# The last triangular inverse moved beside the recurrence, and a layer's modulations moved from one filler to another

## The chip, the cores and the metric

The kernel runs on one core of one Trainium2 chip. The metric is the device time of one execution in microseconds (us). Engines are named as in the profile: PE (TensorE matmul), PEld (its weight load), DVE (VectorE), ACT (ScalarE), POOL (GpSimd) and SP (SyncE, here only a queue that issues transfers).

## The reference

The program is two blocks on 512 latent tokens and 256 context tokens of width 1024, in float32. The first block mixes three branches (window pooling, a differential attention, and a bidirectional recurrence called rwkv), merges them through gates, and ends in a mixture of experts. The second block has two layers: layer 0 is a long convolution (hyena) beside an mLSTM, layer 1 a latent attention, each with a feed-forward part. Each layer's norms and residuals are modulated by vectors computed from a conditioning vector. Cut to what matters here:

```python
def wkv_step(S, inp):                      # the recurrence, token by token
    r, w, k, v, a, b = inp
    sa = jnp.einsum('dbhvk,dbhk->dbhv', S, a)
    S = S * w[..., None, :] + sa[..., None] * b[..., None, :] + v[..., None] * k[..., None, :]
    return S, jnp.einsum('dbhvk,dbhk->dbhv', S, r)

def merge_branches(branches, gates, w_br, w_out):
    g = jax.nn.sigmoid(gates.reshape(B, L, N_BRANCH, D_MODEL))
    merged = g[:, :, 0] * (branches[0] @ w_br[0])
    for n in range(1, N_BRANCH):
        merged = merged + g[:, :, n] * (branches[n] @ w_br[n])
    return merged @ w_out

def ada_mod(cv, w, b):                     # the modulations: 1024 -> 6 * 1024
    m = jax.nn.silu(cv) @ w + b
    return jnp.split(m, N_MOD, axis=-1)
```

## The kernel before

Matrix products are made in float32 by splitting each operand into a high and a low part (names ending in h/hi and l/lo) and adding three products. A split is a cast on ACT and a difference on DVE.

Phase 1 makes the three branches. A first stage runs four generators woven together: `rwkv_inputs` (the recurrence's inputs for four chunks of two heads each), `attend` (the attention), `pools_gates` (pooling, then the modulations of the first block and of layer 0), and `rwkv_blocks`. The last of these inverts, for each chunk, the 32x32 triangular diagonal blocks: 31 steps, each a multiplication and a reduction on DVE over a growing square (`rwkv_block`), then two transposes whose results are stored to memory as `rw_inv`. A chunk's blocks are handed over in the list `todo` by the end of `rwkv_chunk_inputs`; the tiles (blkT, inv, blt, blkO) come from the pool of the recurrence's inputs. The steps of the first three chunks are paced by `PACE`; those of the fourth are not.

Then `rwkv` runs the recurrence: 24 units and 24 steps (four chunks of six pieces of 128 tokens), chunks 0 and 1 side by side and then 2 and 3. A unit (`rwkv_unit`) loads its inputs (ARl and BKl on SP's queue, X from `rw_inv` on POOL's) and prepares matrices that don't depend on the state; a step (`rwkv_step`) carries the state on. At most three units are ahead of the steps. Beside them runs `filler`: the 24 gate projections (`gates`, weights wg in pieces of four 128-row slices) and the merge of the first two branches (`merge_first`, matmuls mp, 16 units). The filler's progress is tied to the share of steps done: a gate i may start when 2 * i is not over `FILL` * (done / 24 + 0.1), a merge unit when 48 + 8 * b + n is not. The pools of the filler lie at the right end of the memory, where later x (the residual) and the second set of constants (const, vec) are put. After the recurrence `rwkv_out` normalises a chunk's result, and `merge` takes the third branch and the output projection.

The modulations are made by `ada_steps`: 96 loads of 256 KB (wada) for a whole layer, one matmul of 32 columns for each, four of them at a time into one PSUM bank, then a copy and eight small matmuls (adc). Those of layer 1 (`ada_w1`) run in `layer0` as the lowest stream beside the long convolution and the mLSTM, with 5 buffers.

The order of the work is decided in two steps. `weave` picks the next generator by a model of the clock in the program (`Clock`): among those whose inputs are modelled as ready, the one with the lowest rank; a stream of rank 2 goes first when the model sees PE too little active. The program's order is then the priority of a list scheduler, which gives each engine the first instruction that it holds to be ready, so the order on an engine can differ from the program's. Each engine and each queue of transfers then runs in that order.

Of the kernel before, what the change touches and what calls it, by code (L numbers as in the profile page):

```python
# [22 lines left out]
FT = mybir.dt.float32  # L23
# [394 lines left out]
class Builder:  # L418
# [288 lines left out]
    def phase1(self, es):  # L707
# [15 lines left out]
        self.fac = self.pool(es, "keep1").tile([128, 4, 2, 6, 2], FT, name="fac")  # L723
        with ExitStack() as e:
            self.h1s = ExitStack()
            hl = self.pool(self.h1s, "h1l", side="right")
            self.h1l = [hl.tile([128, 8, NL], FR, name=n) for n in ("h1l_hi", "h1l_lo")]
            with ExitStack() as e2:
                hc = self.pool(e2, "h1c")
                self.h1c = [hc.tile([128, 8, NCX], FR, name=n) for n in ("h1c_hi", "h1c_lo")]  # L730
                with ExitStack() as e3:
                    self.banks = dict(g=4, s=4)
                    self.psp = self.pool(e3, "psh", 1, space=PSUM)
                    self.head1(e3)
                self.banks = dict(g=3, f=2, s=2, h=1)
                self.psp = self.pool(e2, "ps0", 1, space=PSUM)
                self.lat, self.both = [(*self.h1l, 0, NL)], [(*self.h1c, 0, NCX), (*self.h1l, 0, NL)]
                with ExitStack() as e3, ExitStack() as e4:
                    self.todo = []
                    self.weave(*zip(self.RANKS, (self.rwkv_inputs(e3), self.attend(), self.pools_gates(e4), self.rwkv_blocks())))  # L740
            self.banks = dict(s=7, g=1)
            self.psp = self.pool(e, "ps2", 1, space=PSUM)
            self.rwkv(e)

# [54 lines left out]

    FILL = 64  # L800

    def filler(self, pace):

        with ExitStack() as e:
            yield from self.gates(e, range(self.GATES_A, 24), "g", 2, 4, pace, side="right")
        self.h1s.close()
        with ExitStack() as e:
            yield from self.merge_first(e, pace)

    def merge_first(self, es, pace):  # L810
# [52 lines left out]

    def ada_steps(self, wp, jobs, bufs=ADA):

# [11 lines left out]
        for w, s, L, X in jobs:  # L877
# [4 lines left out]
            nc.vector.tensor_copy(z[:, :, 2 * N - 2:2 * N], s)  # L882
            yield lambda: max(self.after(z), self.room("h"))
            p = self.ps("ada", "h")
            for n in range(N):
                for g in range(0, 8, 4):
                    while len(ahead) < bufs - 1 and todo:
                        load()
                    W = [ahead.pop(0) for _ in range(4)]
                    yield self.after(*W)  # L890
                    for j in range(4):
                        self.mm(p[32 * j:32 * j + 32], z[:, g + j, 2 * (N - 1 - n):2 * (N - 1 - n) + 32], W[j],
                                start=n + g == 0, stop=n == N - 1 and g == 4, skip_group_check=True)
# [322 lines left out]
    def rwkv_inputs(self, es):  # L1216
# [24 lines left out]
        nc.gpsimd.memset(blk, 0.0)  # L1241
        inv = wp.tile([128, 32, 32], FT, name="inv")
        nc.gpsimd.memset(inv, 0.0)
# [13 lines left out]
    def rwkv_chunk_inputs(self, c, proj, pp, W, blk, inv):  # L1257
# [100 lines left out]
        while self.todo:  # L1358
            yield self.later()
        A = pp.tile([128, 32, 32], FT, name="blkT", tag="blkT")  # L1360
        nc.vector.transpose(A, blk)
        self.todo.append((c, pp, A, inv))

    PACE = 1000.0

    def rwkv_blocks(self):

        for _ in range(4):
            while not self.todo:
                yield self.later()  # L1370
            yield from self.rwkv_block(*self.todo[0])
            self.todo.pop()

    def rwkv_block(self, c, pp, A, inv):
        nc = self.nc
        for i in range(1, 32):
            t = pp.tile([128, 31, 31], FT, name="blt", tag="blt")[:, :i, :i]
            nc.vector.tensor_mul(t, inv[:, :i, :i].rearrange("p m j -> p j m"), A[:, i, None, :i].to_broadcast([128, i, i]))
            nc.vector.tensor_reduce(inv[:, i, :i], t, op=OP.add, axis=AX.X)
            yield self.later(self.PACE if c < 3 else 0.0)  # L1380
        for z in range(2):
# [18 lines left out]

    def weave(self, *streams):

# [3 lines left out]
        n = len(S)  # L1406
        while S:
            now = self.clock.free.get("tensor", 0.0)
# [16 lines left out]

    def rwkv(self, es):
        nc = self.nc
# [9 lines left out]
        def units(q):  # L1437
            while todo:
                while made[0] - done[0] >= self.AHEAD:
                    yield self.later()  # L1440
                if todo:
                    c, n = todo.pop(0)
                    made[0] += 1
                    P = {}
                    yield from self.rwkv_unit(c, n, up, q, P)
                    ch[c, n] = P

# [19 lines left out]
        gens = [(0, steps(q)) for q in range(self.LANES)] + [(1, units(q)) for q in range(self.UNITS)]  # L1467
        self.weave(*gens, (2, self.filler(lambda: done[0] / 24 + 0.1)))

# [686 lines left out]
    def layer0(self, es):  # L2156
# [12 lines left out]
        with ExitStack() as e:  # L2169
            self.banks = dict(g=4, n=2, s=1, h=1)  # L2170
            self.psp = self.pool(e, "ps8", 1, space=PSUM)
            ada = self.ada_steps(self.pool(e, "adaw"), [(D["ada_w1"], self.s2, *self.mod2[1])])
            wp = self.pool(e, "ml")
            self.gates_made, self.heads_made, self.heads_out, self.ml, self.mo0, self.mo1, self.mixed = False, 0, 0, None, None, None, [False] * 2
            self.weave((1, self.l0_main()), (0, self.ml_main(wp)), (0, self.ml_heads(0)), (0, self.ml_heads(1)), (2, ada))
        self.dump("mo", self.mo)
# [794 lines left out]
```

## Time and profile before

| | us |
|---|---|
| median of 3 runs | 4022.8 |
| lowest and highest | 4019.8, 4026.1 |
| the profiled execution | 4023.9 |
| its span, first to last instruction | 4022.1 |
| PE busy | 3641.9 (91%) |
| DVE busy | 2487.6 (62%) |
| ACT busy | 1580.0 (39%) |
| mean granted clock of PE | 0.936 |

A busy share is an average over stages with different limits. A line of a timeline gives the start, the duration, the engine (a q behind it is its queue of transfers), the operation with output and input by the program's names, and in square brackets how long the engine sat idle before it and what ended that. The granted clock is 1.0 at 2.4 GHz and 0.5 at 1.2 GHz.

### The profile page before, as it was taken

Reading aid. Unit: us, or ns where it says so; the run is one execution under the profiler, and the core shown is the slowest. Engines: PE = TensorE matmul, PEld = TensorE weight load, DVE = VectorE, ACT = ScalarE, POOL = GpSimd, SP = SyncE. Lnnn points to the kernel's source line nnn. Section 1 sums busy time; section 2 is a strip of 40 time slices with the busy share of each in tenths; the row PEclk is TensorE's granted clock in tenths of the full one; section 3 lists DMA queues with packets and bytes.
Section 4 is the critical chain, followed back from the end, with each engine's and each line's share of the span. In section 5 each row is a group of like instructions: output and inputs, shape, how many; then the busy total and the mean of one; then the engine's idle time right before and its main releaser. Section 6 shows DMA issues by size and latency. Waiting matters only on the chain.

```text
span 4022.1 us, 50169 instructions
## 1 busy us (share of the span) xinstructions
PE 3641.9 (91%) x18332; PEld 2802.5 (70%) x18332; DVE 2487.6 (62%) x4564; ACT 1580.0 (39%) x2765; POOL 510.2 (13%) x742
## 2 busy tenths in 40 slices
PE   8998986898888689999989999899999999999998
PEld 4775443687777466666656886687888877667886
DVE  5597797877877468888874567445423344445343
ACT  3332332333332247666652653224313324434242
POOL 0222111322222021111110000110101000000010
PEclk9998896899888789999999999999999999999999
DMA  5224571322242649999953335312211210012332
GB/s 189 96 84 161 183 255 64 101 79 77 84 132 74 235 184 356 333 335 335 333 217 129 133 105 164 116 35 63 65 61 62 84 55 29 12 42 84 100 95 89
DMA packets 216781, 546.20 MB, mean 136 GB/s; under 512 B 41682, under 2 KB 63859, under 8 KB 189908
## 3 DMA queue, kind: packets, MB, share of 16 engines
q1 hardware_dynamic: 176848, 469.77, 34.1%
q10 hardware_dynamic: 35844, 61.66, 4.2%
q0 software_dynamic: 3840, 11.54, 0.9%
q8 instruction: 146, 2.39, 0.2%
q14 instruction: 103, 0.84, 0.1%
HBM read 490.45 MB, written 52.43 MB: 135 GB/s over the span
## 4 chain that ended last, share of the span: by engine, by line
PE 55%; DVE 6%; DMA 2%; ACT 2%; issue 2%; POOL 1%; another core or an unknown queue 0%; ACTq 0%; SPq 0%; DVEq 0%; POOLq 0%
PE gp L355 34%; PE eg L355 5%; PE ed L355 3%; DVE el L355 2%; PE S L355 2%; PE vp L355 1%; PE eT L355 1%; PE o L355 1%; PE cp L355 1%; PE fk L355 1%; ACT eh L355 1%; PE ada L355 1%; PE mw L355 1%; PE hy L355 1%; PE pt L355 1%
## 5 line engine op out<-in xcount | busy, mean ns | idle before, releaser
L355 ACT CAST wh<-wr 128x512 fp32r<-128x512 f32 (+4 forms) x290 | 190.0, 679 | 579.4 <-PE gp L355 544.9
L355 PE MATMUL gp<-h_hi,wh 128*128 128x512 f32 (+1 forms) x1128 | 402.3, 360 | 5.5 <-ACT h_hi L355 3.0
L355 DVE TENSOR_TENSOR el<-ew,eh 128x1024 fp32r<-128x1024 f32 x284 | 354.1, 1273 | 58.8 <-ACT eh L355 56.1
L355 PE MATMUL gp<-h_lo,wh 128*128 128x512 f32 (+1 forms) x1128 | 387.0, 357 | 0.6 <-DVE h_lo L355 0.3
L355 DVE TENSOR_TENSOR wl<-wr,wh 128x512 fp32r<-128x512 f32 (+4 forms) x290 | 216.2, 765 | 241.4 <-ACT wh L355 239.3
L355 PE MATMUL gp<-h_hi,wl 128*128 128x512 f32 (+1 forms) x1128 | 344.3, 357 | 0.0
L355 ACT CAST eh<-ew 128x1024 fp32r<-128x1024 f32 x288 | 292.8, 1048 | 17.0 <-PE ec L355 10.8
L355 PEld LDWEIGHTS gp<-h_hi,wh 128*128 128x128 f32 x1128 | 213.0, 190 | 55.9 <-ACT h_hi L355 6.6
L355 PEld LDWEIGHTS gp<-h_lo,wh 128*128 128x128 f32 x1128 | 213.7, 190 | 34.2 <-DVE h_lo L355 2.6
L355 PEld LDWEIGHTS gp<-h_hi,wl 128*128 128x128 f32 x1128 | 190.5, 191 | 17.0 <-DVE wl L355 0.3
L355 PE MATMUL ada<-wada,adas 128*32 128x512 f32 (+1 forms) x576 | 166.2, 674 | 32.1 <-DMA wada<-ada_w 17.2
L355 PE MATMUL gp<-z_hi,wh 128*128 128x512 f32 (+1 forms) x528 | 187.8, 356 | 0.0
L355 PE MATMUL eg<-el,xg 128*128 128x512 f32 x384 | 161.9, 422 | 27.0 <-DVE el L355 26.8
L355 PE MATMUL gp<-z_lo,wh 128*128 128x512 f32 (+1 forms) x528 | 179.1, 354 | 0.0
L355 PE MATMUL eg<-eh,xg 128*128 128x512 f32 x384 | 176.4, 459 | 0.1
L355 PE MATMUL gp<-z_hi,wl 128*128 128x512 f32 (+1 forms) x528 | 158.8, 355 | 0.0
L355 POOL MEMSET cvb<- 128x1 f32 x170 | 9.5, 98 | 1059.6 <-DVE fg L355 691.8
L355 PE MATMUL gp<-h_lo,wih 128*128 128x256 f32 (+1 forms) x384 | 132.1, 344 | 0.0
L355 PE MATMUL gp<-h_hi,wih 128*128 128x256 f32 (+1 forms) x384 | 128.9, 356 | 0.0
L355 PEld LDWEIGHTS eg<-el,xg 128*128 128x128 f32 x384 | 72.5, 189 | 69.2 <-DVE el L355 50.4
L355 PE MATMUL eg<-ew,xw 128*128 128x512 f32 x256 | 120.2, 592 | 0.0
L355 PEld LDWEIGHTS gp<-z_hi,wh 128*128 128x128 f32 x528 | 99.1, 188 | 22.7
(860 smaller groups left out, 9481.6 us busy)
## 6 DMA issues: line engine op xcount, KB each, us to landing
ew<-w_exp SPq DMA_DIRECT2D x192, 1024.0 KB, 7.1
wada<-ada_w SPq DMA_DIRECT2D x192, 256.0 KB, 4.4
wr<-ffn_up SPq DMA_DIRECT2D x176, 256.0 KB, 2.6
wada<-w_ada_b SPq DMA_DIRECT2D x64, 256.0 KB, 4.2
wg<-w_in_a SPq DMA_DIRECT2D x48, 256.0 KB, 2.8
wi<-w_in SPq DMA_DIRECT2D x48, 256.0 KB, 2.7
wr<-ffn_dn SPq DMA_DIRECT2D x32, 384.0 KB, 3.1
wr<-ffn_dn SPq DMA_DIRECT2D x32, 320.0 KB, 3.3
```

Of the source, the lines that this page charges most:

```text
L355: return f(*a, **k)
```

## The change

A pool of its own ("blocks") is opened ahead of phase 1's first stage and kept through the recurrence; the inverse's tiles (inv, blkT, blt, blkO) come from it. The first stage's `weave` now ends when all streams but `rwkv_blocks` have ended, and the rest of that stream is woven into the recurrence with rank 0. A unit of chunk c waits in the program until chunk c's inverse has been emitted. The fourth chunk's steps are paced like the others.

The gates' weights come in pieces of two slices in place of four. The modulations of layer 1 leave `layer0` and become the last part of the recurrence's filler, with 9 buffers, in the gates' PSUM bank, and with their own due times; `FILL` goes from 64 to 76. In `layer0` the PSUM bank that they held goes to the small tiles (s from 1 to 2).

```diff
         with ExitStack() as e:
+            self.bp = self.pool(e, "blocks")
+            self.inverted = 0
+            blocks = self.rwkv_blocks()
             self.h1s = ExitStack()
...
-                    self.weave(*zip(self.RANKS, (self.rwkv_inputs(e3), self.attend(), self.pools_gates(e4), self.rwkv_blocks())))
+                    self.weave(*zip(self.RANKS, (self.rwkv_inputs(e3), self.attend(), self.pools_gates(e4), blocks)), keep=blocks)
...
-            self.rwkv(e)
+            self.rwkv(e, blocks)
...
-    FILL = 64
+    FILL = 76
...
-            yield from self.gates(e, range(self.GATES_A, 24), "g", 2, 4, pace, side="right")
+            yield from self.gates(e, range(self.GATES_A, 24), "g", 2, 2, pace, side="right")
...
             yield from self.merge_first(e, pace)
+        with ExitStack() as e:
+            yield from self.ada_steps(self.pool(e, "adaw", side="right"), [(self.D["ada_w1"], self.s2, *self.mod2[1])], 9, "g",
+                                      lambda i: 64 + i / 8 > self.FILL * pace())
...
-    def ada_steps(self, wp, jobs, bufs=ADA):
+    def ada_steps(self, wp, jobs, bufs=ADA, bank="h", wait=lambda i: False):
...
                     yield self.after(*W)
+                    while wait(8 * n + g):
+                        yield self.later()
...
-        inv = wp.tile([128, 32, 32], FT, name="inv")
+        inv = self.bp.tile([128, 32, 32], FT, name="inv")
...
-        A = pp.tile([128, 32, 32], FT, name="blkT", tag="blkT")
+        A = self.bp.tile([128, 32, 32], FT, name="blkT", tag="blkT")
         nc.vector.transpose(A, blk)
-        self.todo.append((c, pp, A, inv))
+        self.todo.append((c, self.bp, A, inv))
...
             self.todo.pop()
+            self.inverted += 1
...
-            yield self.later(self.PACE if c < 3 else 0.0)
+            yield self.later(self.PACE)
...
-    def weave(self, *streams):
+    def weave(self, *streams, keep=None):
...
-        while S:
+        while any(x[3] is not keep for x in S):
...
                     made[0] += 1
+                    while self.inverted <= c:
+                        yield self.later()
...
-        self.weave(*gens, (2, self.filler(lambda: done[0] / 24 + 0.1)))
+        self.weave(*gens, (0, blocks), (2, self.filler(lambda: done[0] / 24 + 0.1)))
...
-            self.banks = dict(g=4, n=2, s=1, h=1)
+            self.banks = dict(g=4, n=2, s=2)
...
-            ada = self.ada_steps(self.pool(e, "adaw"), [(D["ada_w1"], self.s2, *self.mod2[1])])
...
-            self.weave((1, self.l0_main()), (0, self.ml_main(wp)), (0, self.ml_heads(0)), (0, self.ml_heads(1)), (2, ada))
+            self.weave((1, self.l0_main()), (0, self.ml_main(wp)), (0, self.ml_heads(0)), (0, self.ml_heads(1)))
```

## Rows read from the trace of the kernel before

**Rows 1.** Windows: stretch, length, busy PE PEld DVE ACT POOL, clock, DMA share, GB/s

```profile
662.00:712.00 50.00, 24.42 (x70) 14.72 (x69) 45.80 (x99) 8.49 (x22) 1.96 (x2) 0.61 0.11 37
710.00:1310.00 600.00, 518.24 (x3257) 448.57 (x3256) 464.07 (x824) 211.75 (x408) 161.32 (x193) 0.89 0.30 92
2200.00:2440.00 240.00, 238.14 (x1513) 209.55 (x1513) 150.72 (x467) 132.05 (x264) 2.45 (x48) 0.98 0.35 118
2440.00:2600.00 160.00, 138.82 (x747) 98.99 (x746) 93.30 (x205) 47.90 (x99) 15.44 (x26) 0.93 0.48 153
```

**Rows 2.** Timeline of DVE at the end of the first stage

```profile
691.85 0.15 DVE L355 TENSOR_SCALAR ms<-ssum 128x4 f32<-128x4 f32 x1
...
704.69 0.15 DVE L355 SCALAR_TENSOR_TENSOR rsq_y<-rsq_t,rsq_y 128x4 f32<-128x4 f32 x1
...
711.15 1.16 DVE L355 TENSOR_REDUCE inv<-blt 128x31 f32<-128x961 f32 x1
...
712.34 2.10 DVE L355 STREAM_TRANSPOSE blkO<-inv 128x1024 f32<-128x1024 f32 x1
```

**Rows 3.** Timeline of the queues and PE at the recurrence's start

```profile
708.25 0.33 ACTq L355 DMA_DIRECT2D attended<-os  x1
...
721.00 0.96 ACTq L355 DMA_DIRECT2D rw_inv<-blkO  x2
...
724.30 0.33 SPq L355 DMA_DIRECT2D ARl<-rw_ar  x1
...
729.64 0.41 PE L355 MATMUL tkp<-const,BKl 128*128 128x128 f32 x2 [0.58 <-DMA ARl<-rw_ar]
```

**Rows 4.** Windows of tile mp in the recurrence: busy PE, PEld, DVE

```profile
1210.00:1260.00 50.00, 7.53 (x27) 4.82 (x26) 1.36 (x2) 0.76 0.17 53
1260.00:1310.00 50.00, 20.05 (x70) 13.68 (x68) 4.10 (x6) 0.89 0.31 96
```

**Rows 5.** Timeline of ACT: one cast of Us per step

```profile
1197.46 0.37 ACT L355 CAST Us<-pc 128x256 fp32r<-128x256 f32 x1
...
1248.89 0.37 ACT L355 CAST Us<-pc 128x256 fp32r<-128x256 f32 x1 [3.03 <-PE pc L355]
...
1294.13 0.37 ACT L355 CAST Us<-pc 128x256 fp32r<-128x256 f32 x1 [3.41 <-PE pc L355]
```

**Rows 6.** Windows of tile ada in layer 0: busy PE, PEld, ACT

```profile
2200.00:2440.00 240.00, 4.27 (x32) 0.63 (x32) 0.00 (x0) 0.98 0.35 118
2440.00:2600.00 160.00, 25.71 (x96) 4.11 (x96) 0.59 (x1) 0.93 0.48 153
```

**Rows 7.** Tile ada: PE idle before it, in layer 0, then in phase 1

```profile
  DMA wada<-ada_w: 39.3, 28
...
  DMA wada<-ada_w: 18.3, 19
```

**Rows 8.** The chain that ended last, 2200 to 2660 us, by line

```profile
by line: PE gp L355 46.6%; PE fk L355 7.3%; PE mw L355 5.2%; PE mN L355 4.4%; PE ada L355 3.6%; PE gc L355 3.3%; PE hy L355 2.8%; DMA hg<-hy_g 2.0%; DMA wada<-ada_w 1.9%; issue 1.8%; PE mc L355 1.8%; DMA hdec<-hyd 1.4%; DMA mot<-mix 1.3%; D
```

**Rows 9.** Timeline of PE: a convolution's matmul at either clock level

```profile
2589.76 0.41 PE L355 MATMUL fk<-fsl,dft5121h 128*128 128x256 f32 x1
...
2593.65 0.28 PE L355 MATMUL fk<-fch,nyq 128*128 128x256 f32 x1
```

**Rows 10.** Recurrence's end: two pieces of the chain, then timeline of ACT and DVE

```profile
1307.48 2.06 DMA merged<-mgt
...
1310.01 10.35 DMA vec<-vec
...
1313.30 0.63 ACT L355 ACTIVATE gsq<-ysb 128x512 f32<-128x512 f32 x1 [6.78 <-DMA w_r<-w_r]
...
1321.01 0.68 DVE L355 TENSOR_REDUCE gva<-gsq 128x8 f32<-128x512 f32 x1
```

**Rows 11.** Groups by form in the recurrence, DVE: busy, mean ns

```profile
L355 DVE TENSOR_TENSOR wgl<-wg,wgh 128x512 fp32r<-128x512 f32 x45 | 31.4, 701 | 31.1 <-ACT wgh L355 31.0
L355 DVE TENSOR_TENSOR Al<-Mt,Ah 128x256 fp32r<-128x256 f32 x48 | 20.1, 419 | 8.9 <-ACT Ah L355 8.8
```

More of the change, by code (lines that the diff above doesn't have):

```diff
@@ L882, in ada_steps @@
             nc.vector.tensor_copy(z[:, :, 2 * N - 2:2 * N], s)
-            yield lambda: max(self.after(z), self.room("h"))
-            p = self.ps("ada", "h")
+            yield lambda: max(self.after(z), self.room(bank))
+            p = self.ps("ada", bank)
             for n in range(N):
@@ L1424, with rwkv @@
     AHEAD = 3
-    def rwkv(self, es):
+    def rwkv(self, es, blocks):
         nc = self.nc
```

## The prediction

> **What bounds the kernel now.** I read the windows by stage first. The reader is to see there that three stretches are not filled by the engine that does most of the work. From 662 to 712 us, PE is busy for 24.4 of 50 us at a granted clock of 0.61, while DVE is busy for 45.8: the last chunk's triangular inverse runs beside the tail of the attention. In the recurrence (710 to 1310) PE is busy for 518 of 600 us and DVE for 464. In layer 0, PE is 99% busy from 2200 to 2440 and 87% busy from 2440 to 2600 [rows 1]. So DVE ends the first stretch, no engine is full in the second, and the third has a part where every microsecond of PE counts and a part where it does not. Then I read the timelines at the three places the diff touches: the start of the recurrence, its end, and the modulations in layer 0.
>
> **The recurrence's start.** The last inverse ends with its 31st reduction at 711.15 and a transpose at 712.34 [rows 2]. The second transpose's two stores go out at 721.00 on ACT's queue. Only at 724.30 is the first unit's load of ARl issued on SP's queue, and its first matmul (tkp) starts at 729.64 [rows 3]. The attention itself was over at 708.25, when its last store was issued [rows 3]. ARl has nothing to do with the inverse, so it waits for memory: the inverse's tiles lie in the pool that the recurrence reuses. After the change they lie in a pool of their own that outlives the stage, the stage ends with the attention, and only chunk 3's own units wait for that inverse, 12 steps later. What is late next is the attention's last store: 708.25 plus 0.3 of issue plus 2.06 for a store of the same size [rows 10] gives 710.6 in place of 724.3, 13.7 us earlier. The inverse's last reduction and two transposes (1.16 + 2 x 2.10 = 5.4 us of DVE [rows 2]) now run beside the first unit, whose splits queue behind them on DVE; I take 4 us of it. Net: **-9.7 us**. The gate matmuls that filled PE during the old wait lose their cover, but units and gates share a PE that is idle 14% of this stage [rows 1], so I add nothing for them.
> Bounds: 0, if the attention's pools also hold the memory or the gates collide; and -22.5, if in addition the attention's last normalisation, which takes from 691.85 to 704.69 because its tiny instructions alternate with the inverse's long ones [rows 2], collapses, since the inverse's steps are now paced. I do not expect that: a step that comes later in the program still fills DVE whenever the other chain waits.
>
> **Gates fed in half-size pieces.** The gates' weights come as 2 rather than 4 slices: 96 casts and 96 differences of 128x256 in place of 48 of 128x512. On DVE a difference takes 419 ns at 256 columns and 701 at 512 [rows 11]: 96 x 0.419 - 48 x 0.701 = 6.6 us more over the recurrence. ACT has room for its share, and the 48 added issues on SP are spread over 400 us. DVE is 77% busy and often the releaser of PE, so I take half: **+3 us** (bounds 0 and 6.6; the smaller pieces of PE work let a recurrence step in sooner, which could make it -5).
>
> **The modulations leave layer 0.** They are 29.98 us of PE time there, 4.27 in the full stretch and 25.71 in the other [rows 6], and PE sat idle for 39.3 us before them, waiting for their weights [rows 7]. The chain that ended last between 2200 and 2660 gives 3.6% of 460 us to these matmuls and 1.9% to their loads: 16.6 + 8.7 = 25.3 us [rows 8]. The 4.3 in the full stretch count whole. Of the other 21 I take two thirds, since PE is only 87% busy there and loads and evictions of the long convolution become the next wait: 4.3 + 14 = **-18 us**. The 96 loads also leave SP's queue, where the convolution's loads stand behind them; that and the second bank for the small PSUM tiles are the reason to allow as much as -35.
> A matmul of the convolution takes 0.41 us in its lower clock state and 0.28 in the upper [rows 9], and this stretch had a granted clock of 0.93 with the filler in it [rows 1]; without it PE may fall to 1.2 GHz more often. The Trainium skill, in "TensorE: Matmul & The Clock Gate" (Part 1: The HAM clock gate), says that the throttled state is the default and that recent activity releases it; by that rule the stretch would lose clock and this term could shrink to about 0, where by the chain it is -18. That is a rival below.
>
> **The modulations enter the recurrence.** The same 30 us of PE, 96 loads of 256 KB, one memset and a copy now end the filler. With FILL at 76 the last gate is allowed at step 13 instead of 15, the merge's units from 14 to 18 instead of 16 to 22, and the modulations from step 18 to 22. So the filler is denser throughout. Cost if all of it fell into idle time: 0. If none: 30 us, and PE would also wait in order for late weights: 39.3 us per 96 loads with 5 buffers, 18.3 per 160 with 9 [rows 7], so 11 at the 9 buffers used here, 41 in all. Nearest is this pair: from 1197.46 to 1248.89 two steps take 51.4 us, and from 1248.89 to 1294.13 they take 45.2 [rows 5], though the windows at 1210 and 1260 hold 7.5 and 20.1 us of the merge's matmuls [rows 4]. The chain of a unit and a step sets the period there, not the filler. I take **+12 us**, nearer to nothing than to all.
>
> **The recurrence's end.** The merge's last store (2.06 us) ends the right-hand pools, then the second constants land 10.35 us after their issue at 1310.01, and additions that need them stand on DVE in front of the last chunk's variance sum (gva), which starts at 1321.01 although its input (gsq) was made by 1313.9 [rows 10]. After the change the merge's tiles are gone some 60 us earlier and the modulations' pool is smaller (nine 2 KB buffers), so the constants should be there in time: **-7 us**. Bounds: -15, if ACT's queue is also freed (gsq waited there until 1313.30), and +10, if the last modulations run beyond the last step and the loads of x wait for them.
>
> **Sum.** -9.7 + 3 - 18 + 12 - 7 = -19.7 us. The profiled execution took 4023.9 us (span 4022.1), 1.1 above the median 4022.8 of the runs shown; from the median this gives 4003.1, and I say **4003 us**.
>
> **Rivals.** (1) *The modulations choke the recurrence: slower.* Their 25 MB come within about four steps, some 100 us, in which SP's queue also brings ARl and BKl for the last units; a load that waits for one of the nine buffers holds up those behind it, and PE stands in order before late weights. Against it: the windows at 1210 and 1260 leave PE idle. For it: 39.3 us of such idling in layer 0. All other terms make -31.7, so it decides from +40 on, and 41 us is the bound above. The late loads would also spoil the end: with the end's term at 0 the time is 4022.8 - 24.7 + 41 = 4039, with it at +10 it is 4049; I take **4042**. (2) *Cancelled: no change.* Layer 0 keeps its time because its clock falls (-18 becomes 0): **4021**. In the stretch 2440 to 2600, PE does 113 us of other work; by the two rows (0.41 against 0.28, 46% more) a third of it in the lower state costs 17 us [rows 9]. (3) *More than forecast.* The normalisation's alternation goes (-12.8), layer 0 gives the chain's whole 25.3 and the modulations fall into idle time (-12): 4003 - 12.8 - 7.3 - 12 = **3971**. That the inverse does not move is possible too (its steps may be scheduled as before): then the first term still holds, since it rests on memory and not on their order.
>
> **How the numbers follow.** Chances: forecast 0.48, (1) 0.20, (2) 0.20, (3) 0.12. A difference of 0.2% (8 us) is about what a measurement of this kernel can tell from none. Faster: 0.48 + 0.12 = 0.60; same 0.20; slower 0.20. The forecast's own range is 3988 to 4014. The range for all reaches to most of (1) and (3): 3970 to 4038.
>
> **What would show it.** Right: in the changed profile ARl is issued within a few us of the last attended store, and the last inverse's reductions lie beside tkp and m; the ada matmuls lie before 1310 with less than 15 us of PE idle on their weights; vec's load comes well before gva; and the stretch of layer 0 is shorter with a clock near 0.93. Wrong: ARl still waits for something past 720; the steps' period in the last hundred microseconds grows above 51 us; the clock in the convolution falls below 0.85; or x's load holds up the end.

## The result and the profile after

The changed kernel is slower: 4069.0 us (median of 5 runs, 4062.8 to 4076.0) against 4022.8 us. The two medians differ by 46 us. The ratio on record is 1.0100, with a 95% interval from 1.0083 to 1.0116, so about 40 us more. The profiled execution took 4069.7 us (span 4067.9, mean granted clock 0.935) against 4023.9 (4022.1, 0.936). PE is busy for 3663.6 us in place of 3641.9.

The recurrence's start went as forecast. Timeline of the queues, DVE and PE there, in the kernel after; it answers to [rows 2, 3]:

```profile
706.72 0.33 ACTq L355 DMA_DIRECT2D attended<-os  x1
...
710.78 0.33 SPq L355 DMA_DIRECT2D ARl<-rw_ar  x1
...
713.02 1.14 DVE L355 TENSOR_REDUCE inv<-blt 128x31 f32<-128x961 f32 x1
...
714.20 2.04 DVE L355 STREAM_TRANSPOSE blkO<-inv 128x1024 f32<-128x1024 f32 x1
...
715.25 0.38 PE L355 MATMUL tkp<-const,BKl 128*128 128x128 f32 x2
```

ARl is issued 4.1 us after the attention's last store, in place of 16.0 us, and the inverse ends beside the first unit. The other end of the recurrence is where the time went. Timeline there, after; it answers to [rows 10]:

```profile
1295.53 0.37 ACT L355 CAST Us<-pc 128x256 fp32r<-128x256 f32 x1 [0.86 <-PE pc L355]
...
1301.98 0.33 ACTq L355 DMA_DIRECT2D merged<-mgt  x1
...
1303.45 0.69 DVE L355 TENSOR_REDUCE gva<-gsq 128x8 f32<-128x512 f32 x1 [0.74 <-ACT gsq L355]
...
1304.75 2.78 SPq L355 DMA_DIRECT2D wada<-ada_w  x6
...
1382.58 0.35 SPq L355 DMA_DIRECT2D vec<-vec  x1
...
1383.35 2.25 SPq L355 DMA_DIRECT2D wr<-w_br  x3
...
1390.14 0.34 ACTq L355 DMA_DIRECT2D x<-x_t  x1
...
1392.78 0.76 PE L355 MATMUL gp<-br_hi,wh 128*128 128x512 f32 x1 [0.84 <-issue]
```

The first load of a modulation's weight (wada) is issued 2.8 us after the merge's last store, when the last step is over. Only behind the 96th do vec's load and the merge's next weights (wr) follow on SP's queue, and x's load on ACT's. Tile ada in this stretch, after (count: duration in ns least, median, most; first and last start; then what ended the idle time ahead of it, us and times, PE and its weight load added up; it answers to [rows 7]; behind it the same row for PE and for PEld alone):

```profile
L355 PE MATMUL ada<-wada,adas x192: 592/617/1063, 1310.2 to 1387.1; 128*32 128x512 f32 x192
...
  DMA wada<-ada_w: 71.4, 100
```

```profile
  DMA wada<-ada_w: 8.5, 6
...
  DMA wada<-ada_w: 62.9, 94
```

So of the 71.4 us, PE itself stood idle for 8.5 and its weight load for 62.9. PE counts as busy for most of the stretch, but its matmuls start at the pace of the loads: 192 of them take 77 us here, and 23 us in a run told below in which nearly all of their weights are there.

Windows of the same stretch, after, with the columns of [rows 1]:

```profile
1300.00:1350.00 50.00, 32.12 (x86) 6.87 (x86) 9.17 (x24) 3.88 (x6) 4.93 (x5) 0.83 0.95 348
1350.00:1400.00 50.00, 47.97 (x155) 15.88 (x154) 5.42 (x24) 2.33 (x5) 0.00 (x0) 0.93 1.05 398
1400.00:1450.00 50.00, 44.46 (x181) 35.29 (x180) 28.52 (x40) 16.64 (x24) 0.00 (x0) 0.93 0.61 225
```

The transfers fill this stretch: a share of 1.05 and 398 GB/s between 1350 and 1400, with DVE busy for 5.4 of 50 us. It was a loaded stretch before too, since the experts' first weights and the merge's are loaded in it, if not the most loaded: from 1600 to 1700 us the kernel before has a share of 0.92. A window of the kernel before just behind its recurrence:

```profile
1310.00:1360.00 50.00, 14.02 (x40) 10.54 (x41) 11.82 (x36) 7.08 (x12) 3.79 (x3) 0.53 0.83 311
```

In the chain that ended last, between 1300 and 1420 us after (start, duration, what), the modulations stand with their loads, and behind them the merge's weights come late:

```profile
1345.35 32.21 PE ada L355 x94
1377.58 4.98 DMA wada<-ada_w
...
1383.35 4.43 DMA wr<-w_br
...
1393.64 9.76 DMA wr<-w_br
...
1412.46 9.74 DMA wr<-w_out
```

Layer 0 gave nothing back. From its first vp matmul to the feed-forward's first h_hi it lasts 597.9 us (2172.8 to 2770.7), before 598.1 us (2127.8 to 2725.9). Its convolution after, the stretch that answers to the last line of [rows 1]:

```profile
2485.00:2645.00 160.00, 114.92 (x600) 93.96 (x599) 88.64 (x188) 43.97 (x92) 15.77 (x26) 0.79 0.25 79
```

PE is busy for 23.9 us less than before, and the stretch is no shorter; the granted clock is 0.79 in place of 0.93.

**One scale for all kernels.** The profiled executions reach the attention's last store (attended) between 701 and 712 us, so the table gives each event's distance from that store, read from the views by tile of each kernel. The columns behind the first two are experiments, told below. The last w_out load closes what the change touches on this side of layer 0: from it to the end of the span before takes 4022.1 - 708.3 - 682.3 = 2631.5 us, and after 4067.9 - 706.7 - 733.4 = 2627.8 us.

| us after the last attended store | before | after | after_without | inverse_alone | pieces_alone | modulations_before_merge |
|---|---|---|---|---|---|---|
| first load of ARl | 16.0 | 4.1 | 4.1 | 4.1 | 15.4 | 4.1 |
| last cast of Us (last step) | 585.8 | 588.8 | 584.8 | 580.2 | 582.6 | 567.6 |
| last ytp (last chunk normalised) | 617.3 | 601.8 | 598.2 | 595.0 | 598.2 | 579.6 |
| load of x | 601.8 | 683.4 | 594.8 | 582.3 | 607.9 | 653.4 |
| last load of w_out | 682.3 | 733.4 | 670.2 | 660.7 | 674.8 | 705.5 |

So the change has lost 51 us by the last row, all of it behind the last ytp, which still comes 15.5 us earlier than before.

### The profile page after: what moved, and what is told of

It reads as the page before. It is cut to its first block, busy times and chain, and to the rows that moved or that the text cites. A ratio compares the mean times of both kernels' runs of the same rounds, so it can differ in the third digit from the quotient of the medians.

```text
span 4067.9 us, 50471 instructions
## 1 busy us (share of the span) xinstructions
PE 3663.6 (90%) x18332; PEld 2803.9 (69%) x18332; DVE 2492.3 (61%) x4612; ACT 1588.4 (39%) x2814; POOL 508.0 (12%) x742
## 4 chain that ended last, share of the span: by engine, by line
PE 53%; DVE 7%; DMA 3%; ACT 2%; issue 2%; POOL 1%; another core or an unknown queue 0%; ACTq 0%; SPq 0%; DVEq 0%; POOLq 0%
PE gp L355 32%; PE eg L355 5%; PE ed L355 3%; PE S L355 2%; DVE el L355 2%; PE vp L355 1%; PE eT L355 1%; PE o L355 1%; PE cp L355 1%; PE fk L355 1%; PE ada L355 1%; PE hy L355 1%; ACT eh L355 1%; DMA wada<-ada_w 1%; PE mw L355 1%
## 5 line engine op out<-in xcount | busy, mean ns | idle before, releaser
L355 PE MATMUL ada<-wada,adas 128*32 128x512 f32 (+1 forms) x576 | 183.6, 666 | 27.6 <-DMA wada<-ada_w 12.8
L355 PEld LDWEIGHTS ada<-wada,adas 128*32 128x32 f32 (+1 forms) x576 | 31.8, 111 | 137.4 <-DMA wada<-ada_w 77.2
```

The source lines that it names most:

```text
L355: return f(*a, **k)
```

## The experiments

Each time is a median, and each ratio is against runs of the kernel before on the same chip (their medians lay between 4025.8 and 4029.5 us). Theory A: the modulations stand last in a filler that already lasts to the recurrence's end; they run alone behind it and are limited by their loads. Its rival, theory B: the recurrence is slowed by the inverse, the smaller pieces and the fuller filler.

**The parts, one by one.**

*inverse_alone* keeps the inverse's move and the half-size pieces; the modulations go back to layer 0, as in the kernel before.

```diff
-    FILL = 76
+    FILL = 64
...
-        with ExitStack() as e:
-            yield from self.ada_steps(self.pool(e, "adaw", side="right"), ...)
...
+            ada = self.ada_steps(self.pool(e, "adaw"), [(D["ada_w1"], self.s2, *self.mod2[1])])
```

> Only the moved inverse and the half-size gate pieces (which its memory asks for); the modulations stay in layer 0 and FILL stays 64. Theory A (the loss is the place of the modulations: they stand last in a filler that already lasts to the recurrence's end, and run alone after it): no loss is left, and the part of the earlier start that survives is seen, 4005 to 4018 us. Theory B (the loss is the recurrence itself: the inverse and the smaller gate pieces crowd DVE beside the units, and the early start is given back): 4023 us or above, with the last cast of Us at 1294 us or later.

Measured: 3998.3 us, ratio 0.9941 (0.9927 to 0.9954): 24 us less than before, more than theory A allowed, and the fastest kernel of this study. The earlier start is there, and x is loaded at 1283.3 us in place of 1310.1. Timeline of the queues in inverse_alone:

```profile
701.04 0.33 ACTq L355 DMA_DIRECT2D attended<-os  x1
...
705.10 0.33 SPq L355 DMA_DIRECT2D ARl<-rw_ar  x1
...
1283.34 0.39 ACTq L355 DMA_DIRECT2D x<-x_t  x1
```

*modulations_alone* does the other half.

```diff
-    FILL = 64
+    FILL = 76
...
             yield from self.merge_first(e, pace)
+        with ExitStack() as e:
+            yield from self.ada_steps(self.pool(e, "adaw", side="right"), ...)
...
-            ada = self.ada_steps(self.pool(e, "adaw"), [(D["ada_w1"], self.s2, *self.mod2[1])])
```

> Only the modulations move (FILL 76, the inverse and the gate pieces as before). Theory A: their 96 loads begin when the merge's last tile is gone, near 1305 us, and last some 75 us; of these about 30 lie over loads and waits that were there before, so 4060 to 4080 us. Theory B: the move costs little, 4005 to 4030 us.

Measured: 4059.4 us, ratio 1.0086 (1.0072 to 1.0100), 35 us more. The inverse and the smaller pieces are not needed for the loss; the modulations and FILL, the fuller filler of theory B, are left. The loss is a little smaller than expected, since in this order the merge ends at 1260 us, the loads run from 1267 to 1372, and the first of them lie beside the last two steps. The last step itself is late, 620.9 us after the attended store against 585.8. ACT's casts of Us for steps 20, 22 and 24 [rows 5], then the modulations' loads:

```profile
1243.17 0.36 ACT L355 CAST Us<-pc 128x256 fp32r<-128x256 f32 x1
...
1290.79 0.37 ACT L355 CAST Us<-pc 128x256 fp32r<-128x256 f32 x1 [3.76 <-PE pc L355]
...
1331.70 0.37 ACT L355 CAST Us<-pc 128x256 fp32r<-128x256 f32 x1 [2.44 <-PE pc L355]
```

```profile
L355 SPq DMA_DIRECT2D wada<-ada_w x96: 327/382/1392, 1267.1 to 1372.1; - x96
```

The modulations have not made the steps late. Step 20 is late by 43 us already (532.4 after the attended store, before 489.2), 24 us ahead of the first modulation's load, and the last two steps, beside the loads, take 40.9 us in place of 45.2. What is denser up to there is the filler: the merge's matmuls lie from 1085 to 1261 us in place of 1128 to 1303. So in this kernel the fuller filler slows the recurrence. How much of the 35 us is its share isn't known, since FILL at 76 with pieces of four and without the modulations was not run.

*after_without* is the changed kernel without the moved work.

```diff
-        with ExitStack() as e:
-            yield from self.ada_steps(self.pool(e, "adaw", side="right"), ...)
...
+        for t in self.mod2[1]:
+            nc.gpsimd.memset(t, 0.0)
```

> The changed kernel, with layer 1's modulations left out altogether: the inverse, the gate pieces and FILL 76 as in the changed kernel. Theory A: all of the loss goes and the early start is seen, 4000 to 4018 us, and x's loads are issued near 1305 us in place of 1382. Theory B: 4050 us or above, since the recurrence would still be the slow part.

Measured: 4008.7 us, ratio 0.9957 (0.9944 to 0.9969). The whole loss, 1.0100 - 0.9957 = 1.4% or 58 us, is the modulations': the inverse, the pieces and FILL are here as in the kernel after, so theory B is out for that kernel. x is loaded at 1301.8 us in place of 1390.1, and wr follows. Timeline and tile wr of after_without:

```profile
1301.79 0.34 ACTq L355 DMA_DIRECT2D x<-x_t  x1
```

```profile
L355 SPq DMA_DIRECT2D wr<-w_br x8: 327/328/430, 1331.1 to 1349.2; - x8
L355 SPq DMA_DIRECT2D wr<-w_out x8: 327/328/328, 1352.4 to 1377.2; - x8
```

*layer0_without* prices what their absence gives layer 0.

```diff
-            self.banks = dict(g=4, n=2, s=1, h=1)
+            self.banks = dict(g=4, n=2, s=2)
...
-            ada = self.ada_steps(self.pool(e, "adaw"), [(D["ada_w1"], self.s2, *self.mod2[1])])
...
+        for t in self.mod2[1]:
+            nc.gpsimd.memset(t, 0.0)
```

> The kernel before, with layer 1's modulations left out altogether (their vectors are only the bias) and the freed PSUM bank given to the small tiles: it prices what their absence gives layer 0. The forecast's term: 18 us less, 4005 us. Theory A as the trace of after shows it (layer 0 lasts 612 us in both kernels): 4020 to 4025 us.

Measured: 4024.9 us, ratio 0.9994 (0.9983 to 1.0004): 2 us less, with nothing excluded between 7 less and 2 more. The 18 us are not there. Its convolution stretch looks like that of after:

```profile
2440.00:2600.00 160.00, 111.35 (x611) 91.97 (x610) 87.19 (x180) 43.69 (x91) 15.99 (x25) 0.81 0.26 81
```

*pieces_alone* changes one number of the kernel before.

```diff
-            yield from self.gates(e, range(self.GATES_A, 24), "g", 2, 4, pace, side="right")
+            yield from self.gates(e, range(self.GATES_A, 24), "g", 2, 2, pace, side="right")
```

> The kernel before with one number changed: the gates' weights in pieces of two slices in place of four. The forecast's term is +3 us with bounds -5 and 6.6: 4020 to 4032 us. A rival to the reading of inverse_alone (its 28 us less come from the smaller pieces, not from the inverse): 4000 to 4012 us.

Measured: 4015.2 us, ratio 0.9965 (0.9950 to 0.9980): 14 us less, outside the forecast's bounds and on the other side of zero. By the table the steps end 3 us earlier and the last ytp 19 us earlier. The second number goes with the order on DVE, which is another one with this number. Timeline of DVE in pieces_alone:

```profile
1304.59 0.69 DVE L355 TENSOR_REDUCE gva<-gsq 128x8 f32<-128x512 f32 x1 [0.74 <-ACT gsq L355]
...
1320.67 0.21 DVE L355 TENSOR_TENSOR mod20l<-mod20l,vec 128x48 f32<-128x48 f32 x1 [0.27 <-DMA vec<-vec]
```

Before, gva stood behind these additions and their late constants until 1321.01 [rows 10]; here it stands ahead of them. Some of it goes again, since x is loaded 6 us later.

*inverse_fill76* is inverse_alone with one number changed.

```diff
-    FILL = 64
+    FILL = 76
```

> The kernel of inverse_alone with one number changed, FILL 76 in place of 64; the modulations stay in layer 0. inverse_alone took 3998 us and after_without 4009 us, and they differ in FILL and in whether layer 0 has its modulations. Theory A (FILL alone makes these 10 us, by another order of the recurrence's work): 4005 to 4013 us. Theory B (layer 0 without its modulations is what loses them): 3994 to 4002 us.

Measured: 4014.1 us, ratio 0.9970 (0.9956 to 0.9984), against 0.9941 for inverse_alone and 0.9957 for after_without. That is just above theory A's range and far from theory B's. With everything else alike, FILL at 76 costs 12 us; against after_without it would be 6, if layer 0's modulations cost nothing, and the 5 us between that kernel and this one are within the noise. In the trace the merge's last group of matmuls starts 19 us later by the attended store (589.0 against 569.9), and its last store is issued 13 us later (592.4 against 579.8). Why a looser limit makes the merge end later was not followed further.

**What makes the modulations dear.**

*after_four_loads* keeps their matmuls and their place, and takes away the loads.

```diff
             w, n, k = todo.pop(0)
-            W = wp.tile([128, 512], FT, name="wada", tag="wada", bufs=bufs)
-            nc.sync.dma_start(W, w[k][:, n * 512:n * 512 + 512])
+            if bank == "g" and len(kept) == 4:
+                W = kept[k % 4]
+            else:
+                W = wp.tile([128, 512], FT, name="wada", tag="wada", bufs=bufs)
+                nc.sync.dma_start(W, w[k][:, n * 512:n * 512 + 512])
+                kept.append(W)
```

> The changed kernel, but layer 1's modulations use the first four pieces of their weights for all 96 matmuls: 4 loads in place of 96, the same matmuls at the same place. Theory A (the 25 MB of loads set the 80 us between the last step and the merge): 4020 to 4035 us. Theory B (the matmuls and their place in PE's order do): 4055 us or above.

Measured: 4010.7 us, ratio 0.9961 (0.9943 to 0.9979), close to the kernel without any modulations (0.9957). It is better than theory A asked. The loads cost 1.0100 - 0.9961 = 1.4% or 56 of the 58 us. What is left for the matmuls behind the last step is 2 us, with nothing excluded between 7 less and 10 more; in the profiles this kernel's last load of w_out comes 680.2 us after the attended store, 10 later than in after_without. Tile ada and the last loads in this kernel:

```profile
L355 PE MATMUL ada<-wada,adas x192: 592/592/1063, 1315.9 to 1338.7; 128*32 128x512 f32 x192
...
  DMA wada<-ada_w: 1.2, 3
```

```profile
L355 SPq DMA_DIRECT2D wr<-w_out x8: 327/328/328, 1365.0 to 1389.1; - x8
```

They now take 23 us, while the merge waits for its own weights. The 96 loads are 25.2 MB; at the 385 GB/s that after moves in most of the time from 1330 to 1380 us that is 65 us, close to the 56.

*modulations_before_merge* exchanges the filler's last two parts.

```diff
         with ExitStack() as e:
+            yield from self.ada_steps(self.pool(e, "adaw", side="right"), [(self.D["ada_w1"], self.s2, *self.mod2[1])], 9, "g")
+        with ExitStack() as e:
             yield from self.merge_first(e, pace)
-        with ExitStack() as e:
-            yield from self.ada_steps(self.pool(e, "adaw", side="right"), ...)
```

> The changed kernel with the filler's last two parts exchanged: the modulations run between the gates and the merge, with 9 buffers and no due times, so that their loads lie inside the recurrence. Theory A (the filler already lasts to the recurrence's end, and what is put anywhere in it lengthens it): the merge is pushed behind the last step, 4040 to 4075 us. Theory B (only their place at the very end is wrong, where their loads run alone): 4005 to 4020 us.

Measured: 4049.3 us, ratio 1.0064 (1.0040 to 1.0087): 26 us more than before, theory A's answer. Tile ada (the idle time is again PE's and its weight load's), a window, and tile mp of this kernel:

```profile
L355 PE MATMUL ada<-wada,adas x192: 589/593/619, 1113.1 to 1230.2; 128*32 128x512 f32 x192
...
  DMA wada<-ada_w: 4.4, 5
```

```profile
1100.00:1200.00 100.00, 92.35 (x663) 62.41 (x661) 74.16 (x136) 31.72 (x66) 23.53 (x29) 1.00 0.70 234
```

```profile
L355 PE MATMUL mp<-mb_hi,wbh x64: 387/397/797, 1243.2 to 1350.2; 128*128 128x512 f32 x64
```

This is the most telling run. In this place the modulations do the steps no harm: PE and its weight load wait 4.4 us for their weights, the granted clock is 1.00 from 1100 to 1200 us, and the last step comes 21 us earlier than in the kernel after (567.6 against 588.8). But the merge now starts at 1243 us, and its last group of matmuls comes 56 us later than in after_without (644.5 against 588.4 us after the attended store). In this order, too, the recurrence has no time for all three parts of the filler one after the other, and against after_without the modulations cost 1.0064 - 0.9957 = 1.1% or 43 us. To run the last two parts side by side was not tried.

**Layer 0.**

*layer0_four_loads* keeps the modulations' matmuls in layer 0 and loads only four pieces.

```diff
+            if len(jobs) == 1 and len(kept) == 4:
+                W = kept[k % 4]
+            else:
```

> The kernel before, but layer 1's modulations (in layer 0) use four pieces of their weights for all matmuls: PE keeps this work there, and the loads are gone. layer0_without, where both are gone, took the time of before. Theory A (the convolution's own chain of loads, evictions and short matmuls sets this stretch, and the modulations lie in its gaps): 4019 to 4028 us. Theory B (without them PE's clock falls and eats a real gain of some 15 us; with the matmuls kept and the loads gone the gain would show): 4005 to 4015 us.

Measured: 4029.5 us, ratio 1.0003 (0.9988 to 1.0019). It was meant to tell a lost clock from a chain, and does not: with the weights there, the matmuls went early, to the layer's start, and layer 0 took 606.7 us in place of 598.1. Tile ada in this kernel:

```profile
L355 PE MATMUL ada<-wada,adas x192: 592/592/1063, 2099.7 to 2140.5; 128*32 128x512 f32 x192
```

*layer0_late_four* was to hold them back in the program.

```diff
+                    while len(jobs) == 1 and not self.l0_made:
+                        yield self.later()
```

> As layer0_four_loads, but the modulations' matmuls wait in the program until layer 0's projections are made, so that they lie in the convolution's stretch as in the kernel before (in layer0_four_loads they ran at 2100 to 2140 us, and layer 0 took 606.7 us in place of 598.1). Theory A (that stretch is set by its own chain): layer 0 takes 595 to 600 us and the kernel the time of before, 4022 to 4030 us. Theory B (without the modulations the gain is there and the falling clock eats it; here the clock stays near 0.93 and nothing is loaded): layer 0 takes 590 us or less, 4010 to 4018 us.

Measured: 4031.8 us, ratio 1.0008 (0.9996 to 1.0020), layer 0 604.7 us. The scheduler again put most of them early, and the convolution had a clock of 0.81:

```profile
L355 PE MATMUL ada<-wada,adas x192: 592/592/1063, 2108.5 to 2468.5; 128*32 128x512 f32 x192
```

So this question stays open. What both show beside it: in the kernel before, where the matmuls wait for late loads, half of them lie in the convolution [rows 6], and *layer0_without* finds no cost of them there. With the weights there early, layer 0 is 7 to 9 us longer in the two profiles; the timed ratios give 1 and 3 us more, and both intervals hold none as well as 8.

**The inverse and the recurrence's end.**

*inverse_unpaced* is inverse_alone with the fourth chunk's steps placed as before.

```diff
-            yield self.later(self.PACE)
+            yield self.later(self.PACE if c < 3 else 0.0)
```

> The kernel of inverse_alone, with the fourth chunk's steps unpaced as in the kernel before: the tiles keep their own pool, but the program places the inverse as early as before, beside the attention. Theory A (the gain comes from memory: ARl's load waited for the inverse's tiles; where the inverse's steps stand does not matter): the time of inverse_alone, 3992 to 4004 us, and ARl's first load within 6 us of the last attended store. Theory B (the gain comes from the steps' later place): half of it or more is gone, 4010 us or above.

Measured: 4008.2 us, ratio 0.9958 (0.9942 to 0.9973), between the two expectations. ARl's first load comes 2.1 us after the attended store:

```profile
707.01 0.33 ACTq L355 DMA_DIRECT2D attended<-os  x1
...
709.14 0.33 SPq L355 DMA_DIRECT2D ARl<-rw_ar  x1
```

Both transposes of the inverse come behind that load (710.4 and 718.6 us), and it no longer waits for them. So the wait at the start did rest on memory, and not on where the inverse stands. By the attended store its last w_out load is no later than inverse_alone's (658.9 against 660.7 us), while the timed ratios lean the other way with intervals that overlap. Whether the pacing is worth anything is undecided.

*inverse_two_bg* tried to go further: bg's second load at the recurrence's end gets a tile of its own.

```diff
+        g2 = self.bp.tile([128, 31, 31], FT, name="blt", tag="blt").rearrange("p i j -> p (i j)")[:, :NL]
+        nc.sync.dma_start(g2, self.d_bg[c][:, 1])
...
-        bg = pp.tile([128, NL], FT, name="bg", tag="gsq")
-        nc.sync.dma_start(bg, self.d_bg[c][:, 1])
-        nc.gpsimd.tensor_mul(yo, yo, bg)
+        nc.gpsimd.tensor_mul(yo, yo, g2)
```

> The kernel of inverse_alone, with a second buffer for the output factor bg at the recurrence's end: its two loads use one tile there, so the second is issued after POOL's addition at 1298.61 us and POOL waits 8.55 us for it before the multiplication that ends the branch. With the tile that the inverse left (blt) both are issued together. If this wait stands on the path that sets the merge's start: 6 to 9 us less than inverse_alone, 3986 to 3994 us. If the merge waits for other loads then (wr, mg): 3995 to 4002 us.

Measured: 4016.1 us, ratio 0.9972 (0.9957 to 0.9986), slower than inverse_alone, and outside both expectations. The wait itself is gone; timeline of POOL, where the second operation follows the first at once:

```profile
1297.79 1.27 POOL L355 TENSOR_TENSOR yo<-yo,bg 128x512 f32<-128x512 f32 x1 [5.64 <-ACT yo L355]
1299.14 1.29 POOL L355 TENSOR_TENSOR yo<-yo,blt 128x512 f32<-128x512 f32 x1
```

But the loads changed the order of the whole recurrence: the merge's last matmuls start at 1300.6 us, 589.6 after the attended store, as in inverse_fill76 (589.0) and not as in inverse_alone (569.9), and x is loaded 17 us later by that mark. The five kernels with the smaller pieces and with the modulations in layer 0 lie 11 to 24 us below before. How much of inverse_alone's lead is the inverse and how much a lucky order can't be told from them.

## Why the prediction was wrong

The sign was wrong, and the time lies above the range. By its own terms:

| term | forecast, us | measured, us |
|---|---|---|
| the recurrence's start | -9.7 | ARl -11.9; left at the last step: +3.0 in after, -5.6 in inverse_alone |
| smaller pieces | +3 | -14 (-20 to -8) |
| modulations leave layer 0 | -18 | -2 (-7 to +2) |
| modulations enter the recurrence | +12 | +58 in after, +43 ahead of the merge; FILL at 76 another 6 to 12 |
| the recurrence's end | -7 | last Us to last ytp 31.5, after 13.0: -18.5 |

**The step that failed** is "the modulations from step 18 to 22", and with it the +12 us of that term. I took the limits that FILL sets for the times at which the filler runs. They are the earliest times, and the filler was late already. The order in which the program emits its work shows it; what each kernel emits (steps done when the unit is emitted, and the step from which FILL allowed it; the forecast had 14 for the merge's first unit):

```text
                   before          after               modulations_alone
gate 24            16 (from 15)    16 (from 13)        13 (from 13)
merge, unit 1      17 (from 16)    18 (from 13)        13 (from 13)
merge, unit 16     24 (from 22)    24 (from 18)        21 (from 18)
first modulation   in layer 0      behind 24 (from 18) 21 (from 18)
```

The last column is FILL at 76 with the old pieces of four slices: there the filler does follow the looser limit. With pieces of two it does not: inverse_fill76 emits at 16, 18 and 24 too, and so does, for its last unit, the program of modulations_alone when it is given pieces of two (24, worked out from the program, not run). So two parts of the change worked against each other; why the smaller pieces hold the filler back was not followed. An earlier place would not have saved the forecast: modulations_alone still lost 35 us, part of it by a recurrence that the denser filler slowed, and modulations_before_merge, whose modulations are emitted from step 16 on, 26.

The forecast had the row that said so. Between 1260 and 1310 us the merge still ran 70 matmuls [rows 4], although the last Us of step 22 is at 1248.89 [rows 5] and FILL allowed the last unit then. A filler that ends with the recurrence leaves no room behind it, whatever PE's idle share is. I read the same rows as idle PE.

**The price was mis-sized as well.** The forecast counted waits by the number of buffers and put the bound of the whole term at 41 us. Both rows were misread there. The 39.3 us are not PE's idle time but PE's and its weight load's together, 13.1 and 26.2; and the 18.3 us [rows 7] belong to the 96 loads of ada_w alone, not to 160, so that by the forecast's own way the bound is 30 + 18.3 = 48. It falls short of 58 all the same. The four-load run shows that nearly all of the cost is in the bytes. The bound from the trace would have been bytes over rate, in the stretch where the loads would fall if they came late: 25.2 MB at 311 to 398 GB/s, 63 to 81 us. Rival 1 had the right sign, a place close to the right one ("the last modulations run beyond the last step" stood as a bound of the end's term), and a price too small by 17 us (41 for what cost 58). Its mechanism, late weights that hold up the steps, is not what happened in the kernel after, whose last step is 3 us late by the attended store. In modulations_before_merge the steps went faster beside the modulations, and in modulations_alone the last two took 40.9 us beside them, in place of 45.2.

**Layer 0 was rival 2's.** The forecast took two thirds of 21 us because the chain of waits passes through ada [rows 8]. It counted 128 of the 192 matmuls: the other 64, 20.3 us of PE, lie from 2101 to 2196 us, ahead of both stretches that it priced. Even so nothing was gained. A chain shows what ran last, and when that work is gone, what waited beside it takes its place: the stretch keeps its length and PE's idle time grows from 21.2 to 45.1 of 160 us. The clock fell as rival 2 said, from 0.93 to 0.79. The Trainium skill, in "TensorE: Matmul & The Clock Gate" (Part 1: The HAM clock gate), says that recent activity releases the clock from its lower state; the trace agrees with that, 0.79 to 0.81 in every kernel looked at whose convolution had no modulations in it, or in layer0_late_four few. Whether the length is set by that clock or by the convolution's own loads and evictions was not settled.

**The start was right in its cause, not in its worth.** ARl came when the attention's last store was out, and it rested on memory, as the unpaced run shows. What is late next was missed: the steps of chunks 0 to 3 and the filler share PE and DVE in a list-scheduled order, and at the last step 5 to 12 us separate inverse_alone (580.2 after the attended store) from kernels that differ from it in one number (585.7 with FILL 76, 568.6 unpaced). With FILL at 76, as in the kernel after, nothing of the 11.9 us was left there.

**The end's term came, and by another way.** gva no longer stood behind vec: in after it starts at 1303.45 while vec's load is issued at 1382.58. That gave 15.5 us up to the last ytp. It came without the reason that the forecast gave, a merge that ends 60 us earlier: by the attended store the merge's last store is issued 4 us earlier (595.3 against 599.2). And pieces_alone, which changes only the pieces, has nearly the same gain (31.5 us to 15.6), so it is luck of the order.

Of the listed signs, ARl's was right. "The ada matmuls lie before 1310" failed (1310.2 to 1387.1), as did vec's load ahead of gva and the layer's shorter stretch. "Less than 15 us of PE idle on their weights" failed as the forecast read that row (71.4 us), while PE alone has 8.5: the sign was a poor one. Of the signs for wrong, x's load did hold up the end, and the clock in the convolution fell below 0.85 (0.79).

## What to carry to other kernels

Before work is appended to a filler, look where the filler's last piece runs now, not at when it may run: if it ends with the stage, the new work comes behind the stage. Price moved loads in bytes against the transfer share of the stretch in which they land, and PE's share separately: here no cost was found for late weights in a convolution with a share of 0.48, and the same bytes behind the recurrence, where the share was 0.83 already, cost 56 us. Before an idle time is put down to an engine, see whether the row adds up two. And test the parts of a change one by one: here the inverse's move and the smaller pieces were worth 24 us together, the moved modulations cost 58, and the pieces, changed in passing and forecast at +3, gave 14 alone.

## What the runs showed of the hardware

Over 50 us the core's transfers moved 398 GB/s at a share of 1.05, where the kernel before, just behind its recurrence (1310 to 1360 us), had 311 at 0.83. The Trainium skill, in "Perfetto Trace Analysis" (Engine Utilization, Roofline), gives 358 GB/s as a core's share of the memory and says that a core alone can pull more, up to some 435 GB/s by its 16 engines; the trace agrees. In the chain of after, one weight of the merge issued there takes 4.43 us to land (1383.35) and one issued 10 us later 9.76 (1393.64).

The small matmuls of the modulations (32 columns of weights) beside the recurrence went with a granted clock of 1.00 from 1100 to 1200 us; with the gates' and the merge's matmuls there, the kernel before had 0.79 from 1100 to 1150 and 0.96 from 1150 to 1200. Over these 100 us PE was busy for 92.35 in the one and for 88.39 in the other. Whether the better clock comes from the kind of filler or from PE's fewer gaps was not told apart.
